# Two hybrid decoder layers on one core: the state-key transposes of layer 0 at one place, the attention's third tile at the place of the spatial gating

## The chip, the core and the metric

The kernel runs on one core of a Trainium2 chip. In this kernel TensorE (PE in the profile) does the matrix products and transposes, with results in PSUM; VectorE (DVE) and ScalarE (ACT) take them from there and do the elementwise work; GpSimd (POOL) has small operations on statistics; SyncE (SP) issues the DMAs. The metric is the device time of one execution in microseconds. Before the change the median of three runs is 1480.12 us (1479.88 to 1480.13).

## What is computed

Two decoder layers over one sequence of 2048 tokens, 1024 wide, float32. Layer 0, cut to what matters here:

```python
h = x @ w_in
q, k, v, g_a, a_lr, u, sv, g_b = _split(h, EVEN_SIZES)
log_a = jax.nn.log_sigmoid((a_lr @ w_a2 + b_a).astype(jnp.float32)) / GLA_TAU
o = _gla(...)                                   # gated linear attention, 4 heads, chunks of 64
o_a = _head_rmsnorm(o, gla_norm_g) * jax.nn.silu(g_a)
o_b = _spatial_gating(gelu(u), gelu(sv), ...) * jax.nn.silu(g_b)   # 4 groups, chunks of 128
y = jnp.concatenate([o_a, o_b], axis=-1) @ w_out
x = _layer_norm(DN_ALPHA * x + y, ln_g, ln_b)
```

In the gated linear attention the state that enters a chunk of 64 tokens is the decayed state before it plus a product of keys and values of the chunk before; each chunk also has causal scores of its own. Layer 1 has the same outline with retention and pooling in place of the two branches.

## The kernel before

The sequence is taken in four blocks of 512 tokens (`for b in range(NB)`, line 852), each through layer 0 and then layer 1. A block is four tiles of 128 tokens, and a tile holds two chunks of the attention.

**The large products.** `unit` (line 164) multiplies the block by 512 columns of a weight matrix. Operands are cut into a high and a low part, and three products of the parts are added (`PASSES`, line 162), so each of the 8 slices of the contraction takes three instructions per result; these are the matmuls of line 181. In most units the work goes in two halves of two results each (width 2): a half is 8 slices by 2 results by 3 passes, 48 matmuls. Each result has one of four PSUM banks named `big`. The weights come by DMA; `cut` (line 114) makes the high part on ScalarE (line 89) and the remainder on VectorE (line 90), and `pace` (line 124) spreads these cuts over the matmuls.

**The small work and its places.** All other work of TensorE is put between the large products by a list of steps. `later(fn, delay)` appends a step; `between()` (line 147) takes one off every delay and runs those that have come to zero, in the order in which they were appended. A unit of width 2 calls `between()` four times: in the middle of its first half, at that half's end once the results have been handed to ScalarE or VectorE, in the middle of the second half and at its end. The text calls these its places 1 to 4. Every engine takes its instructions in the order in which they are written here.

Layer 0 has the units in this order: values (two), q and k, sv, "u and gate" (groups 0 and 1 of the spatial gating), the attention's gate, the rest of u and gate, and then two for the output. The steps around the change:

| step | lines | place before | PSUM that it takes |
|---|---|---|---|
| `state_keys`, pair of heads 0: four transposes, four ScalarE copies | 555 to 560 | q and k, 3 | one `tr` bank |
| `state_keys`, pair of heads 1 | 555 to 560 | sv, 1 | one `tr` bank |
| `first`: scores and chunk states of tile 0 | 422 | sv, 2 | two `s` banks, two `tr` banks |
| `outputs(0)` | 428 | sv, 3 | the same |
| `outputs(1)` | 428 | u and gate, 1 | the same |
| `outputs(2)`, the third tile | 428 | u and gate, 3 | the same |
| `sgu(0)`, `sgu(1)`, the spatial gating's first products | 625 | u and gate, 4 | one `tr` bank each |
| `outputs(3)` | 428 | attention's gate, 1 | two `s` banks |
| `out` of heads 0 and 1 | 653 | attention's gate, 2 | one `tr` bank each |

`outputs(t)` writes the products of tile t, then the scores and the chunk states of tile t + 1 (line 442). The chunk states lie in two banks u[0] and u[1] from `tr()`. `carry_on` (line 410) then adds them to the running states with four VectorE sums (line 414) that read u[0], u[1], u[0], u[1] in this order. Behind them come the norm (ScalarE squares of line 583, a VectorE sum of line 585, GpSimd's power of line 201), `prepare` (lines 418 and 575) and the scaling (line 591).

`sgu(g)` (line 625) takes a bank from `tr()`, fills it with four float32 products that have the normalised `zt` as weights (line 629, two instructions each), and then has three VectorE operations, the second of which reads that bank (lines 630 to 634).

There are **two banks** behind `tr()`:

```python
    ps_tr = ctx.enter_context(tc.tile_pool(name="ps_tr", bufs=2, space=PSUM))
```

A third request must wait until the last reader of the bank that comes round again is done; the framework puts that wait on the TensorE instruction that first writes it.

In block 0 alone, `angles(2)` (line 327) spreads 21 operations of the rotary tables over seven places, three at each, from sv, place 2, to "u and gate", place 4. The sixth group, at place 3 of "u and gate", is a clamp on VectorE, a sine on ScalarE that reads it and a negation on VectorE.

Of the kernel before, what the change touches and what calls it, by code (L numbers as in the profile page):

```python
# [51 lines left out]
def trunk(ctx, tc, x, xT, pos, wv, w, w_a2, pvec, rowp, sgu_rows, w_sT, w_pool, ropec, poolc, out):  # L52
# [24 lines left out]
    def tr():  # L77
        return ps_tr.tile([P, 4, P], F32, tag="tr", name="trp")
# [65 lines left out]
    def later(fn, delay=1):  # L144
        steps.append([delay, fn])
# [112 lines left out]
    s0 = const.tile([P, 2, P], F32, name="s0")  # L258
# [29 lines left out]
    for kt in range(KT):  # L288
# [4 lines left out]
        t = wpool.tile([P, 2, 512], F32R, tag="w", name="wt")  # L293
# [64 lines left out]
    def half(n):  # L358
        return slice(64 * n, 64 * n + 64)
# [3 lines left out]
    def by_heads(copy, dst, src):  # L363

        for r in range(2):
            for c in range(2):
                copy(r, dst(r, c), src(c, r))
# [10 lines left out]
    def attend(qk, kt, vt, state, upd, norm, delays):  # L378

        states = [state, s_odd]

        def mm(dst, lhsT, rhs, start=False, stop=False):
            nc.tensor.matmul(dst, lhsT=lhsT, rhs=rhs, start=start, stop=stop, skip_group_check=True)  # L385

        def banks():

            return [ps_s.tile([P, 4, P], F32, tag="s", name="att") for _ in range(2)]

        def vals(t, s, r, c):
            return vt(t)[half(r), (2 * c + s) * P:(2 * c + s + 1) * P]

        def scores(t, ps, start):
            for c in range(2):
                for s in range(2):
                    for r in range(2):
                        k, q = qk(s, 64 * r, t)
                        mm(ps[r][half(r), 2 + c, half(s)], k[:, half(c)], q[:, half(c)],
                           start=start and c == 0 and s == 0, stop=True)  # L400

        def chunk_states(t):
            u = [tr(), tr()]
            for s in range(2):
                for c in range(2):
                    for r in range(2):
                        mm(u[r][half(c), s, :], kt(s, r, c, t), vals(t, s, r, c), start=s == 0, stop=True)
            return u

        def carry_on(t, u):  # L410
            after = states[(t + 1) % 2]
            for dst, src, c in ((s_mid, states[t % 2], 0), (after, s_mid, 1)):
                for r in range(2):
                    nc.vector.tensor_tensor(dst[half(r)], src[half(r)], u[r][half(c), 0:2, :], op=ALU.add)

        def prepare(t, ps):
            for r in range(2):
                nc.vector.copy_predicated(pm[t % 2][half(r)], mask_b[half(r)],
                                          ps[r][half(r), 2:4, :].rearrange("p c (s i) -> p (c s) i", i=64))
            upd(t, states[(t + 1) % 2])  # L420

        def first():
            ps = banks()
            scores(0, ps, True)
            carry_on(0, chunk_states(0))
            prepare(0, ps)

        def outputs(t):
            m, ps = pm[t % 2], banks()
            last = t == NT - 1  # L430
            for s in range(2):
                for c in range(2):
                    for r in range(2):
                        mm(ps[r][half(c), s, :], m[half(r), 2 * c + s, :], vals(t, s, r, c), start=s == 0)
            for s in range(2):
                for c in range(2):
                    for r in range(2):
                        mm(ps[r][half(c), s, :], qk(s, 64 * r, t)[1][:, half(c)],
                           (states[t % 2], s_mid)[c][half(r), s, :], stop=True)
            if not last:  # L440
                scores(t + 1, ps, False)
                carry_on(t + 1, chunk_states(t + 1))
            scale = norm(t, [p_[:, 0:2, :] for p_ in ps])
            if not last:
                prepare(t + 1, ps)
            scale()

        later(first, delays[0])
        for t in range(NT):
            later(lambda t=t: outputs(t), delays[t + 1])  # L450
# [40 lines left out]
    def layer0(b, xs):  # L491

        vt = r8.tile([P, NT, 512], F32, tag="r8", name="v0")
# [49 lines left out]
        def evac_qk(n, ps):  # L543
            held[n] = ps
            if n % 2 == 0:
                return
            s = n // 2
            psq, psk = held[n - 1], ps

            G = r8.tile([P, 3, TB], F32, tag="r8", name=f"G{s}")  # L550
            e, ei, _ = decays[s]
            nc.vector.tensor_tensor(G[:, 1, :], psk, ei, op=ALU.mult)
            nc.vector.tensor_tensor(G[:, 0, :], psq, e, op=ALU.mult)

            def state_keys():
                pt = tr()
                for t in range(NT):
                    nc.tensor.transpose(pt[:, t, :], G[:, 1, t * P:(t + 1) * P], ident)  # L558
                kt4 = G[:, 2, :].rearrange("p (t c i) -> p t c i", c=2, i=64)
                by_heads(act_copy, lambda r, c: kt4[half(r), :, c, :], lambda c, r: pt[half(c), :, half(r)])  # L560

            later(state_keys, 2)
            heads[s] = G

        unit(xs, evac_qk, False)

        def qk(s, b0, t):
# [25 lines left out]
            return scale  # L593


        attend(qk, kt, lambda t: vt[:, t, :], s0, upd, norm, (2, 3, 5, 7, 9))
        if b == 0:
            angles(2)
        zt = z8.tile([P, NT, 512], F32, tag="z8", name="zt")
# [252 lines left out]
    for b in range(NB):  # L852
        x1, rows = layer0(b, list(xunits))
        layer1(b, x1, rows)
# [68 lines left out]
```

## Time and profile before

| | |
|---|---|
| median of three runs | 1480.12 us |
| the profiled execution's own time | 1480.69 us |
| its span, first to last instruction | 1479.0 us |
| granted TensorE clock, mean | 0.997 |
| busy: PE, DVE, ACT, POOL | 99%, 67%, 40%, 7% of the span |
| line 181 on PE, all 6144 matmuls | 725.2 + 625.7 us of modelled busy time |
| DMA | 162.35 MB, mean 110 GB/s |

A PE matmul is recorded with a modelled end, and matmuls overlap, so the busy share says little about the rate. The chain of waits is of more use: it cuts overlapping matmuls at the start of the next and gives the time for which each kind of work held the path to the end. In its rows stand the start, the length, the engine, the tile written, the line and the number of instructions. A row of the timeline gives start, length, engine, line, operation, written and read tile, and in brackets the engine's idle time before it with what ended it.

### The profile page before, as it was taken

What the parts mean: (1) busy time and instruction counts of PE and PEld (TensorE: products, weight loads), DVE (VectorE), ACT (ScalarE), POOL (GpSimd) and SP (SyncE); (2) the same over time, 40 slices, a digit from 0 to 9 for tenths busy, and PEclk for the clock granted to TensorE, in tenths of its full rate; (3) what the DMA queues carried; (4) which work ended last, traced back from release to release, by engine and by line L of the source; (5) the groups of instructions that cost most, each with busy time, mean ns of one, the idle gap of its engine ahead of it and who ended that gap; (6) DMA issues with size and microseconds to landing.
All of it is one profiled execution on the core that took longest, in us unless ns stands there. A gap on an engine that the chain in (4) does not pass through costs nothing.

```text
span 1479.0 us, 23323 instructions
## 1 busy us (share of the span) xinstructions
PE 1463.8 (99%) x8752; PEld 1224.1 (83%) x8752; DVE 989.7 (67%) x2056; ACT 595.6 (40%) x1116; POOL 101.0 (7%) x137
## 2 busy tenths in 40 slices
PE   8999999999999999999999999999999999999997
PEld 7888888888988888888898888888889888888886
DVE  5596586757657458676756746967675664696755
ACT  6534424243653332434274342334327434143430
POOL 1010010100001001000100100000010010000001
PEclk9999999999999999999999999999999999999999
DMA  7324423115513341313452243132434325222321
GB/s 240 101 77 152 129 71 111 62 58 173 200 58 114 116 142 57 115 58 98 146 185 86 87 142 114 59 114 75 129 120 164 100 73 175 82 93 80 103 77 57
DMA packets 87057, 162.35 MB, mean 110 GB/s; under 512 B 10096, under 2 KB 18336, under 8 KB 86944
## 3 DMA queue, kind: packets, MB, share of 16 engines
q1 hardware_dynamic: 86944, 160.85, 34.2%
q8 instruction: 69, 1.13, 0.3%
q14 instruction: 44, 0.36, 0.1%
HBM read 152.43 MB, written 8.39 MB: 109 GB/s over the span
## 4 chain that ended last, share of the span: by engine, by line
PE 98%; issue 0%; DVE 0%; DMA 0%; ACT 0%; POOLq 0%; POOL 0%; DVEq 0%; ACTq 0%
PE big L181 89%; PE att L385 3%; PE trp L385 1%; PE trp L629 1%; PE trp L681 1%; PE trp L781 1%; PE trp L656 0%; PE trp L821 0%; PE trp L721 0%; PE trp L558 0%; DMA xraw<-in_xT 0%; PE trp L458 0%; PE trp L514 0%; POOLq L919 0%; POOL lnrs L201 0%
## 5 line engine op out<-in xcount | busy, mean ns | idle before, releaser
L181 PE MATMUL big<-wt,T 128*128 128x512 f32 (+2 forms) x3456 | 725.2, 369 | 6.7 <-ACT wt L89 4.5
L181 PEld LDWEIGHTS big<-wt,T 128*128 128x128 f32 x3456 | 599.1, 190 | 112.3 <-ACT wt L89 4.5
L181 PE MATMUL big<-T,wt 128*128 128x512 f32 x2688 | 625.7, 391 | 0.0
L181 PEld LDWEIGHTS big<-T,wt 128*128 128x128 f32 x2688 | 500.6, 188 | 107.7 <-issue 5.4
L90 DVE TENSOR_TENSOR wt<-raw,wt 128x512 fp32r<-128x512 f32 (+1 forms) x496 | 315.5, 673 | 215.5 <-ACT wt L89 215.1
L89 ACT ACTIVATE wt<-raw 128x512 fp32r<-128x512 f32 (+1 forms) x496 | 296.6, 615 | 312.4 <-PE big L181 214.3
L201 POOL TENSOR_TENSOR lnrs<-lnrs,neghalf 128x1 f32<-128x1 f32 x32 | 40.8, 1275 | 628.0 <-DVE lnrs L198 628.0
L219 DVE SCALAR_TENSOR_TENSOR rows<-rows,big 128x512 f32<-128x512 f32 x64 | 43.6, 682 | 53.1 <-PE big L181 53.1
L370 ACT ACTIVATE v<-big 64x128 f32<-64x128 f32 (+1 forms) x184 | 56.8, 309 | 36.2 <-PE big L181 20.8
L201 POOL TENSOR_TENSOR rs<-rs,neghalf 128x4 f32<-128x4 f32 x48 | 48.9, 1018 | 239.1 <-DVE rs L198 236.5
L683 ACT ACTIVATE T<-trp 128x512 fp32r<-128x512 f32 x32 | 17.4, 596 | 105.6 <-PE trp L681 105.6
L231 DVE SCALAR_TENSOR_TENSOR rows<-rows,lnrs,ln 128x1024 f32<-128x1024 f32 (+1 forms) x36 | 41.6, 1166 | 11.4 <-POOL lnrs L201 10.6
L220 DVE BATCH_NORM_STATS2 lnst<-rows 128x6 f32<-128x512 f32 x64 | 44.5, 695 | 2.2
L228 DVE SCALAR_TENSOR_TENSOR rows<-rows,lnmv,ln 128x1024 f32<-128x1024 f32 x32 | 40.9, 1277 | 0.0
L789 ACT ACTIVATE pb<-big 128x512 f32<-128x512 f32 x16 | 9.6, 600 | 76.7 <-PE big L181 76.2
L90 DVE TENSOR_TENSOR T<-y,T 128x512 fp32r<-128x512 f32 x48 | 31.7, 690 | 12.2 <-ACT T L89 11.7
L641 ACT ACTIVATE act<-big 128x512 f32<-128x512 f32 x32 | 18.3, 598 | 51.2 <-PE big L181 50.5
L607 DVE BATCH_NORM_STATS2 st<-zt 128x6 f32<-128x128 f32 x64 | 13.9, 279 | 35.1 <-ACT zt L603 35.1
L206 DVE SCALAR_TENSOR_TENSOR y<-trp,pv,sg 128x512 f32<-128x512 f32 x48 | 33.7, 745 | 4.4 <-PE trp L656 4.4
L796 DVE TENSOR_TENSOR pl<-pb 128x527 f32<-128x527 f32 x16 | 11.3, 705 | 30.0 <-ACT pb L789 29.9
L89 ACT ACTIVATE T<-y 128x512 fp32r<-128x512 f32 x48 | 28.9, 626 | 6.0 <-DVE y L206 5.7
L90 DVE TENSOR_TENSOR T<-xraw,T 128x512 fp32r<-128x512 f32 x32 | 21.2, 685 | 13.3 <-ACT T L89 13.3
(197 smaller groups left out, 960.6 us busy)
## 6 DMA issues: line engine op xcount, KB each, us to landing
raw<-in_w SPq DMA_DIRECT2D x448, 256.0 KB, 2.9
xraw<-in_xT SPq DMA_DIRECT2D x32, 256.0 KB, 3.1
rows<-in_x SPq DMA_DIRECT2D x8, 1024.0 KB, 7.2
ln<-in_rowp SPq DMA_DIRECT2D x16, 512.0 KB, 6.0
out<-rows SPq DMA_DIRECT2D x12, 512.0 KB, 2.7
raw<-in_wv SPq DMA_DIRECT2D x32, 136.0 KB, 3.0
raw<-in_wv SPq DMA_DIRECT2D x32, 128.0 KB, 2.8
out<-rows SPq DMA_DIRECT2D x8, 256.0 KB, 2.0
```

Of the source, the lines that this page charges most:

```text
L89: nc.scalar.activation(hi, src, AF.Copy)
L90: nc.vector.tensor_tensor(lo, src, hi.bitcast(F32), op=ALU.subtract)
L181: nc.tensor.matmul(p_, lhsT=lhsT, rhs=rhs, start=(kt == 0 and q == 0), stop=(kt == KT - 1 and q == 2))
L201: nc.gpsimd.tensor_tensor(dst, dst, neghalf[:, :n], op=ALU.pow)
L206: nc.vector.scalar_tensor_tensor(y, psT, gain, sil, op0=ALU.mult, op1=ALU.mult)
L219: nc.vector.scalar_tensor_tensor(rh, rh, ALPHA, ps, op0=ALU.mult, op1=ALU.add)
L220: nc.vector.bn_stats(sts[t][:, half, :], rh)
L228: nc.vector.scalar_tensor_tensor(row, row, mv[:, 0:1], gt, op0=ALU.subtract, op1=ALU.mult)
L231: nc.vector.scalar_tensor_tensor(row[:, cs], row[:, cs], rs, bt[:, cs], op0=ALU.mult, op1=ALU.add)
L370: nc.scalar.activation(dst, src, AF.Copy)
L385: nc.tensor.matmul(dst, lhsT=lhsT, rhs=rhs, start=start, stop=stop, skip_group_check=True)
L641: nc.scalar.activation(dst, ps, AF.Silu if kind == "g" else AF.Gelu_apprx_tanh)
```

## The change

```diff
@@ layer0, evac_qk
-            later(state_keys, 2)
+            later(state_keys, 4 - 2 * s)
@@ layer0
-        attend(qk, kt, lambda t: vt[:, t, :], s0, upd, norm, (2, 3, 5, 7, 9))
+        attend(qk, kt, lambda t: vt[:, t, :], s0, upd, norm, (2, 3, 5, 8, 9))
```

No operation is added or removed. For the first pair of heads (s = 0) the state keys get a delay of 4 in place of 2: they leave "q and k", place 3, and come to sv, place 1, directly ahead of those of the second pair, whose delay stays 2. The five delays given to `attend` are those of `first` and of `outputs(0)` to `outputs(3)`; the fourth goes from 7 to 8, so `outputs(2)` leaves "u and gate", place 3, and comes to place 4. There it was appended before `sgu(0)` and `sgu(1)`, so it runs ahead of them (in block 0 with the seventh group of `angles` between). Layer 1 calls `attend` with delays of its own and is not touched.

## The prediction

> **What bounds the kernel now.** I read the page's busy times first, then the list of who waited for whom, cut to TensorE, then the chain of waits in block 1, where the change sits.
>
> ```profile
> PE 1463.8 (99%) x8752; PEld 1224.1 (83%) x8752; DVE 989.7 (67%) x2056; ACT 595.6 (40%) x1116; POOL 101.0 (7%) x137
> ...
> PE 98%; issue 0%; DVE 0%; DMA 0%; ACT 0%; POOLq 0%; POOL 0%; DVEq 0%; ACTq 0%
> ```
>
> ```profile
> PE big L181 <- ACT wt L89: 4.5, 1, 4.5
> PE big L181 <- DVE v L373: 2.1, 2, 1.1
> PE trp L458 <- DVE cst L325: 0.4, 1, 0.4
> PE big L181 <- DVE wt L90: 0.2, 1, 0.2
> ```
>
> TensorE holds 98% of the path to the end, and all its waits for other engines come to 7.2 us, in five pieces. So a microsecond of TensorE work that is saved comes off the end, and a microsecond for which TensorE is made to wait is added to it, since no later wait is there to absorb it. The four other engines matter only through the waits that they cause.
>
> ```profile
> 418.51 0.44 PE trp L558 x4
> 418.94 10.91 PE big L181 x48
> 429.86 0.44 PE trp L558 x4
> ...
> 468.58 1.42 PE att L385 x45
> ...
> 470.51 5.66 PE big L181 x24
> 476.18 1.78 PE trp L629 x16
> 477.96 5.46 PE big L181 x24
> ```
>
> This is the path in block 1. Rows of L558 are the state keys, first at "q and k", place 3, then at sv, place 1. At 468.58 the third tile starts (u and gate, place 3), and at 476.18 the spatial gating's products (place 4), 5.66 us of large products later. No row of another engine stands between: TensorE goes through all places without a stop.
>
> **The state keys.** The change moves four transposes, 0.44 us, to a place that already has four. What could be saved is the cost of one visit. The rows show none: four transposes hold the path for 0.44 us, 0.11 us each, and the 48 large products behind them take 10.91 us, where twice the undisturbed 5.46 us for 24 (477.96) is 10.92. So moving them gives 0.0 us. What hides the copies:
>
> ```profile
> 430.33 1.55 ACT L370 ACTIVATE G<-trp 64x256 f32<-64x256 f32 x4 [5.25 <-PE trp L558]
> ...
> 435.14 1.28 ACT L603 ACTIVATE zt<-big 128x512 f32<-128x512 f32 x2 [1.96 <-PE big L181]
> ```
>
> ScalarE stood idle for 5.25 us before the second pair's copies and for 1.96 us before its next evacuation. Four more copies, 1.55 us, start as early and fit into the 1.96 us, so that evacuation isn't late, and the chunk states of `first`, which need both pairs' copies and both `tr` banks, come after that evacuation's large products. If that cover were gone, the price would be at most the 1.55 us per block; I take nothing. At "q and k", place 3, ScalarE gets 1.55 us back, which nobody waits for.
>
> **The third tile at place 4.** On TensorE the same instructions are issued in another order. The visit of the attention costs something at its exit: 24 large products take 5.66 us behind it and 5.46 us behind the spatial gating, 0.20 us more. In the new order the spatial gating's products stand behind the attention and would pay that 0.20 us in the large products' place. So without any wait the sum is 0.0 us, and at best 0.20 us per block less.
>
> But place 4 now asks for four `tr` banks where there are two: u[0] and u[1] for the chunk states of tile 3, then one each for `sgu(0)` and `sgu(1)`. The first product of `sgu(0)` must wait until u[0] has been read for the last time, by the third of the four sums of L414.
>
> ```profile
> 470.44 5.73 PE L181 MATMUL big<-T,wt 128*128 128x512 f32 x24
> ```
>
> ```profile
> 469.28 0.69 DVE L90 TENSOR_TENSOR wt<-raw,wt 128x512 fp32r<-128x512 f32 x1 [0.66 <-ACT wt L89]
> 470.56 0.86 DVE L414 TENSOR_TENSOR s_mid<-s_odd,trp 64x256 f32<-64x256 f32 x2 [0.60 <-PE trp L385]
> 471.46 0.88 DVE L414 TENSOR_TENSOR s<-s_mid,trp 64x256 f32<-64x256 f32 x2
> ...
> 474.49 0.76 DVE L591 TENSOR_TENSOR v<-att,rs 128x256 f32<-128x256 f32 x2
> ```
>
> At today's place the instruction behind the chunk states starts at 470.44, 1.86 us after the visit began. The sums start at 470.56; the third is the first half of the row at 471.46 and ends at 471.46 + 0.44 = 471.90. Today these banks are next wanted by the spatial gating at 476.18, so nobody waits. How a wait of this kind ends is shown by the one that the trace has, at block 0's constants, where a `tr` bank is asked for while VectorE still reads it:
>
> ```profile
> 36.14 0.69 DVE L325 TENSOR_TENSOR cst<-trp,sgubs 128x512 f32<-128x512 f32 x1 [0.85 <-PE trp L324]
> 36.88 0.18 PEld L458 LDWEIGHTS trp<-alrT,wa 48*128 48x128 f32 x1 [0.67 <-DVE cst L325]
> 36.88 0.50 PE L458 MATMUL trp<-alrT,wa 48*128 48x512 f32 x1 [0.35 <-DVE cst L325]
> ```
>
> VectorE ends at 36.83 and TensorE goes on at 36.88, 0.05 us later. So the spatial gating starts at 471.95 in place of 470.44: **1.51 us** of wait. `sgu(1)` needs u[1], free 0.44 us later, while `sgu(0)` itself takes half of 1.78 us: no second wait. The weight load waits too, since it starts at 36.88 with its matmul; the 0.20 us therefore stays behind the wait. [...] Its ends: 1.31 us by the best exit above, and 2.20 us if one remainder of a cut (0.69 us) lies before the sums. Today the remainder before them ended 0.60 us before they could start; the cuts follow the large products' own steps, place 4 has the same distance to them as place 3, and so I take 1.51 us for blocks 1, 2 and 3: 4.53 us.
>
> What is queued behind: on TensorE the spatial gating and all large products; on VectorE the norm, `prepare` and the scaling of tile 2, then the spatial gating's operations. The fourth tile needs the scaling done, which ends at 475.25, 6.67 us after the visit began. In the new order its visit comes 1.86 + 1.51 + 1.78 + 5.46 = 10.6 us after, so the shorter distance costs nothing.
>
> **Block 0** differs, since VectorE is behind there with the rotary tables.
>
> ```profile
> 103.98 1.42 PE att L385 x45
> ```
>
> ```profile
> 108.72 0.85 DVE L414 TENSOR_TENSOR s_mid<-s_odd,trp 64x256 f32<-64x256 f32 x2
> ...
> 113.29 0.42 DVE L333 TENSOR_SCALAR ang<-ang 128x512 f32<-128x512 f32 x1
> ...
> 114.93 2.50 DVE L90 TENSOR_TENSOR wt<-raw,wt 128x512 fp32r<-128x512 f32 x4 [0.76 <-ACT wt L89]
> 117.35 0.68 DVE L333 TENSOR_TENSOR kk<-kk,ang 128x512 f32<-128x512 f32 x1
> ```
>
> The third tile started at 103.98, yet its sums started at 108.72, without a pause on VectorE before them. With `outputs(2)` gone from place 3, the clamp (113.29 today) takes that slot, 108.72. The four remainders follow it by 1.64 us (113.29 to 114.93, as ScalarE first takes the sine), so 110.36, and the next operation follows by 2.42 us: the sums start at 112.78. The third ends 1.34 us after the first begins (470.56 to 471.90), at 114.12, and TensorE goes on at 114.17. It would have been there at 103.98 + 5.46 + 1.86 = 111.30. The wait is **2.87 us**; its ends are 1.51 us, as in the other blocks, and 4.27 us, if the sums lag as far behind TensorE as today (from 103.98 + 1.86 to 108.72, 2.88 us, and then 1.34 and 0.05). I take the reckoned value, as each of its steps is a row of this stretch.
>
> The waits sum to 4.53 + 2.87 = 7.40 us.
>
> **The clock.** A wait of this length may do more than its own time:
>
> ```profile
> 20.20 0.59 PE L181 MATMUL big<-wt,T 128*128 128x256 f32 x3 [1.01 <-DVE v L373]
> 21.89 2.51 PE L181 MATMUL big<-wt,T 128*128 128x256 f32 x14 [1.10 <-DVE v L373]
> ```
>
> ```profile
> 22.00:24.00 2.00, 2.00 (x14) 2.00 (x15) 1.25 (x7) 0.60 (x3) 1.03 (x4) 0.72 0.93 266
> 24.00:26.00 2.00, 2.00 (x11) 2.00 (x11) 1.36 (x5) 1.99 (x6) 0.00 (x0) 0.50 0.98 317
> 26.00:28.00 2.00, 2.00 (x17) 2.00 (x17) 2.00 (x4) 0.58 (x2) 0.00 (x0) 0.92 0.63 212
> ```
>
> After two waits of 1.01 and 1.10 us with 0.59 us of work between, the granted clock (the third number from the end) fell to half: for 2 × 0.28/0.5 = 1.12 us of the first stretch, all of the second and 0.32 us of the third, 3.44 us in all. Work at half rate for 3.44 us loses 1.72 us. Block 0's 2.87 us is more idle time than the 2.11 us that brought this about; 1.51 us is less. So I count one such drop, in block 0: 7.40 + 1.72 = 9.12 us. Against the profiled execution's own 1480.69 us that is 1489.8 us. The median of the runs lies 0.57 us below that execution, at 1480.12 us, so **1489.2 us**.
>
> **Rivals.** The clock holds: only a longer pause lowers it, the waits alone count, 7.40 us, 1487.5 us. For it: the one drop came after two pauses, and no row shows that a single one brings it about. Against it: 2.87 us is longer than both together. [...]
>
> The clock drops in several blocks: 1.51 us suffices, at up to 1.72 us each. All four: 7.40 + 4 × 1.72 = 14.3 us, 1494.4 us. For it: nothing in the trace shows that 1.51 us is too little. Against it: the only drop seen came after 2.11 us.
>
> Not slower: the wait is covered, and the exit of the attention goes from the path, since the spatial gating's weight loads lie under it. That gives 4 × 0.20 = 0.8 us, 1479.3 us. It decides if the wait per block is under 0.20 us, so if the sums of u[0] were over by the time the chunk states' last products are issued. Against it: the sums can't start before those products (470.56 against 470.44), and three of them take 1.34 us.
>
> A knock-on: VectorE's later work, 1.5 to 2.9 us of TensorE's time closer together, makes a later place wait too. If each block lost its copies' 1.55 us once more on top of the forecast, 1489.2 + 6.2 = 1495.4 us. The 10.6 against 6.67 us above speak against it.
>
> **Chances.** Forecast 0.45, clock holds 0.25, clock drops in several blocks 0.17, not slower 0.08, knock-on 0.05. The range goes from waits at their low end, 4 × 1.31 = 5.2 us, 1485.3 us, to the lower clock in every block, 1494.4 us; the last two cases are left out. About 0.2% (3.0 us) is what a measurement of this kernel can tell from no change. All cases but one are slower by more; the one is 0.06 for no change and, as the exit could be worth more than seen, 0.02 for faster.
>
> **What would show it.** In the profile after, the chain at place 4 of "u and gate" should have a VectorE row of L414, near 1.4 us, between the attention and L629, in each block, and the list of waits a row of L629 waiting for L414, four times, some 7 us in total, the longest in block 0; the granted clock should show one stretch of half rate near 114 us. The state keys should be eight transposes of 0.87 us at one place with no wait at `first`. I am wrong if L629 starts within 0.2 us of the chunk states' end, if the wait in blocks 1 to 3 is over 2.2 us, or if the time moves by another wait than this.

## The result and the profile after

The kernel after takes 1489.68 us, median of four runs (1487.67 to 1490.55), against 1480.12 us before: a ratio of 1.0061, with a 95% interval of 1.0049 to 1.0072. It is slower by 9.6 us. The profiled execution is the one of 1490.55 us, with a span of 1488.8 us; it lies 9.86 us above the profiled execution of before (1480.69 us).

Busy time and the shares of the chain by engine, from the page:

```profile
PE 1466.1 (98%) x8752; PEld 1226.1 (82%) x8752; DVE 990.3 (67%) x2056; ACT 595.3 (40%) x1116; POOL 101.0 (7%) x137
...
PE 95%; DVE 3%; DMA 1%; issue 1%; ACT 0%; POOLq 0%; POOL 0%; DVEq 0%; ACTq 0%
```

The instruction counts are those of before. What is new is that VectorE holds 3% of the path to the end, where it held none. That share, some 40 us, isn't the loss: in block 0 the chain, once it has reached VectorE, goes back almost entirely on that engine from 113.58 to 70.69 us, where VectorE is behind, and 36 us of the share lie there. What TensorE lost is read from its waits. The list of waits, for TensorE alone, names the place (columns: total us, times, longest):

```profile
PE trp L629 <- DVE s L414: 7.4, 4, 2.8
PE big L181 <- ACT wt L89: 4.4, 1, 4.4
PE big L181 <- DVE v L373: 1.8, 2, 1.1
PE big L181 <- DVE wt L90: 0.7, 2, 0.5
PE trp L458 <- DVE cst L325: 0.4, 1, 0.4
```

The first row is the only new one: the spatial gating's products wait for the sums of L414, once per block, 7.4 us in all. In the chain of waits of block 1 it looks like this:

```profile
479.25 1.42 PE att L385 x45
480.67 0.02 PE trp L385
480.69 0.06 PE att L385 x2
480.75 0.51 PE trp L385 x14
481.26 0.39 DVE s_mid L414
481.65 0.03 issue
481.68 0.43 DVE s_mid L414
482.11 0.02 issue
482.13 0.43 DVE s L414
482.56 0.14 issue
482.70 2.02 PE trp L629 x16
484.72 5.50 PE big L181 x24
```

The path leaves TensorE behind the last chunk state, goes through exactly three sums and comes back. The third is the last reading of u[0]; the fourth isn't on the path. The 0.20 us that the large products paid behind the attention is now paid by the spatial gating: its 16 instructions hold 2.02 us (1.78 before), and the 24 large products 5.50 us (5.66 before).

In block 0 the granted clock also falls. The windows of the kernel after (the third number from the end is the clock):

```profile
112.00:116.00 4.00, 2.28 (x11) 2.31 (x12) 3.50 (x8) 2.33 (x5) 0.77 (x2) 0.63 0.73 243
116.00:120.00 4.00, 4.00 (x14) 3.42 (x14) 3.89 (x8) 0.63 (x1) 0.43 (x1) 0.51 0.04 14
120.00:124.00 4.00, 4.00 (x19) 3.05 (x17) 2.23 (x4) 0.00 (x0) 0.00 (x0) 1.00 0.00 0
```

That is 4 × 0.37/0.5 + 4 × 0.49/0.5 = 6.9 us at half rate; the trace's clock record has 0.50 from 113.06 to 119.88 us. What it costs stands in the chain of block 0:

```profile
113.72 3.75 PE trp L629 x16
117.47 6.63 PE big L181 x24
```

These forty instructions hold 10.38 us here and 2.02 + 5.50 = 7.52 us in block 1: 2.86 us for the clock. In blocks 1 to 3 it stays at full rate in this execution, 1.00 from 124 to 1485 us.

The start also took a little less than in the profiled execution of before: the drop of the clock at 22 to 26 us that the prediction shows isn't in this one, which was granted 1.00 from 20 to 28 us. The same eight instructions in the chain of the kernel after, and of the kernel before:

```profile
34.75 0.91 PE trp L324 x8
```

```profile
35.20 0.91 PE trp L324 x8
```

The sum of this execution: 7.4 us of waits, 2.9 us for the clock in block 0, and 0.45 us less at the start. That is 9.85 us, and 9.86 us were measured.

### The profile page after: what moved, and what is told of

The parts are those of the page before. It is cut to its first block, busy times and chain, and to the rows that moved or that the text cites. A ratio compares the mean times of both kernels' runs of the same rounds, so it can differ in the third digit from the quotient of the medians.

```text
span 1488.8 us, 23321 instructions
## 1 busy us (share of the span) xinstructions
PE 1466.1 (98%) x8752; PEld 1226.1 (82%) x8752; DVE 990.3 (67%) x2056; ACT 595.3 (40%) x1116; POOL 101.0 (7%) x137
## 4 chain that ended last, share of the span: by engine, by line
PE 95%; DVE 3%; DMA 1%; issue 1%; ACT 0%; POOLq 0%; POOL 0%; DVEq 0%; ACTq 0%
PE big L181 86%; PE att L385 3%; PE trp L629 1%; PE trp L681 1%; PE trp L385 1%; PE trp L781 1%; DMA raw<-in_w 1%; DVE wt L90 1%; PE trp L821 0%; PE trp L721 0%; PE trp L656 0%; DVE s_mid L414 0%; DVE ang L333 0%; DVE zt L616 0%; PE trp L558 0%
## 5 line engine op out<-in xcount | busy, mean ns | idle before, releaser
L90 DVE TENSOR_TENSOR wt<-raw,wt 128x512 fp32r<-128x512 f32 (+1 forms) x496 | 316.3, 671 | 222.1 <-ACT wt L89 221.5
L90 DVE TENSOR_TENSOR T<-y,T 128x512 fp32r<-128x512 f32 x48 | 31.7, 689 | 12.2 <-ACT T L89 11.8
L583 ACT ACTIVATE sq<-att 128x256 f32<-128x256 f32 x32 | 10.6, 385 | 56.2 <-PE att L385 56.2
```

The source lines that it names most:

```text
L90: nc.vector.tensor_tensor(lo, src, hi.bitcast(F32), op=ALU.subtract)
```

## The experiments

The theory after the result: all of the loss comes from the two transpose banks, named `tr` in the program. The wait for them is set by the third sum, and block 0's wait, the only one over 2 us, lowers the clock as well. The rivals: the order or the number of visits on TensorE costs by itself, moving the keys has a part in it, or the clock falls for another reason in block 0. Each experiment is told with its edit, against the kernel before in the first two and against the full change in the others.

**The keys alone.**

```diff
-            later(state_keys, 2)
+            later(state_keys, 4 - 2 * s)
```

> Only the first line of the change: the state keys of both pairs at one place, the third tile where it was. If a visit of TensorE costs only its own transposes, as the 0.44 us for four and 0.87 us for eight say, this is no change: 1480.1 us, within 0.5 us, with no wait at the tile's first step. The rival, that each visit has a cost beyond its instructions, gives 0.2 us or more per block less, 1479.3 us or lower. If the eight copies in a row made ScalarE late, up to 1.55 us per block more, 1486 us.

1480.43 us (11 runs) against 1480.40 us (21 runs): ratio 1.0000, 0.9991 to 1.0009. In the chain of block 1 the eight transposes stand at one place:

```profile
429.56 0.87 PE trp L558 x8
430.44 5.47 PE big L181 x24
435.90 0.55 PE att L385 x13
```

Eight take 0.87 us, two visits of four took 2 × 0.44 us, and the tile's first step follows without a wait. Merging two visits of this kind gives nothing.

**The tile alone.**

```diff
-        attend(qk, kt, lambda t: vt[:, t, :], s0, upd, norm, (2, 3, 5, 7, 9))
+        attend(qk, kt, lambda t: vt[:, t, :], s0, upd, norm, (2, 3, 5, 8, 9))
```

> Only the second line of the change: the third tile at the place of the spatial gating, the state keys where they were. If the wait for the two transpose banks is the whole loss, the time of the full change comes back: 1487.5 us with the clock held, 1489 to 1490.6 us with a clock drop in block 0, and the list of waits shows L629 behind L414 four times, about 7.4 us. If moving the keys had part in it, it lies between.

1489.47 us (1487.57 to 1490.27), ratio 1.0057, 1.0045 to 1.0070: the time of the full change. The list of waits:

```profile
PE trp L629 <- DVE s L414: 7.4, 4, 2.9
```

Its profiled execution took 1487.68 us, and there the clock held in block 0, although the wait was as long:

```profile
112.00:116.00 4.00, 2.43 (x19) 2.36 (x20) 3.50 (x9) 2.17 (x5) 0.93 (x2) 1.00 0.76 258
116.00:120.00 4.00, 4.00 (x19) 3.29 (x18) 3.90 (x8) 0.63 (x1) 0.27 (x1) 1.00 0.00 0
```

So this execution shows the waits alone: 1480.40 + 7.4 = 1487.8 us. The second edit is the whole loss. The scatter of 1487.6 to 1490.3 us goes with the clock: the two short runs (1487.57 and 1487.68 us) have a mean granted clock of 0.998, the three long ones 0.996 to 0.997. Only one of them was profiled.

**Other banks for the spatial gating.** The wait is taken away by giving `sgu(0)` and `sgu(1)` other banks, with the order unchanged:

```diff
-            pt = tr()
+            pt = big().rearrange("p (t c) -> p t c", c=P) if g < 2 else tr()
```

> The full change, but the spatial gating's first two products take two of the four banks of the large products in place of the transpose banks. The theory: no wait of L629 for L414, no clock drop in block 0, and the time is back near 1480.1 us; in block 0 the next large products may wait up to 1.1 us for ScalarE's evacuation, since their banks are now the two last used: 1480 to 1481.3 us. The rival, that the order itself costs (the spatial gating's products directly behind the attention's), leaves it near 1487.5 us.

1480.97 us (1480.66 to 1481.43, 11 runs), ratio 1.0004, 0.9995 to 1.0013: not shown to differ from the kernel before. The list of waits has no row of L629; the one new row is the predicted one of block 0, and its 0.5 us is about what the two medians differ by (0.57 us). In the profiled execution the clock holds in block 0: the 24 large products behind that wait hold 5.75 us in the chain, against 6.63 us in the full change. The row of the wait:

```profile
PE big L181 <- ACT act L641: 0.5, 1, 0.5
```

In the chain of block 1 the spatial gating now follows the chunk states without a stop:

```profile
476.02 0.44 PE trp L385 x14
476.46 1.98 PE big L629 x16
478.45 5.47 PE big L181 x24
```

The order itself costs nothing that can be measured, and it gains nothing: the 0.20 us at the attention's exit is still there, in the 1.98 us of L629. Two visits merged per block, with no wait left, are worth nothing that can be measured here.

**Both readings of u[0] first.** This shortens the wait by one sum without removing it:

```diff
-            for dst, src, c in ((s_mid, states[t % 2], 0), (after, s_mid, 1)):
-                for r in range(2):
+            for r in range(2):
+                for dst, src, c in ((s_mid, states[t % 2], 0), (after, s_mid, 1)):
```

> The full change, with the four sums in another order: both readings of u[0] first, then both of u[1]. If the spatial gating waits for the last reading of u[0], its wait shortens by one sum, 0.44 us, in each block: 1.07 us in blocks 1 to 3, 2.44 us in block 0, 5.65 us in all, so 1485.8 us with the clock held and up to 1488.7 us with a drop. If it waits for all four sums or for something else behind them, nothing changes: 1487.5 to 1490.6 us.

1488.08 us (1485.72 to 1488.41), ratio 1.0047, 1.0035 to 1.0060. The list of waits and the chain of block 1:

```profile
PE trp L629 <- DVE s L414: 5.6, 4, 2.4
```

```profile
480.37 0.42 DVE s_mid L414
480.79 0.02 issue
480.81 0.43 DVE s L414
481.25 0.14 issue
481.39 2.04 PE trp L629 x16
```

Two sums on the path in place of three, and 5.6 us in place of 7.4. The wait goes with the last reader of the bank. The waits alone would give 1480.40 + 5.6 = 1486.0 us, near the fastest run, 1485.72 us; the profiled execution, 1488.41 us, has a clock drop in block 0, with 0.79 granted from 112 to 116 us and 0.78 from 116 to 120 us. As a whole this version isn't shown to differ from the full change, since their ranges meet: the 1.8 us saved is smaller than the scatter of its runs.

**Block 0 alone, and blocks 1 to 3 alone.** Two kernels:

```diff
-        attend(qk, kt, lambda t: vt[:, t, :], s0, upd, norm, (2, 3, 5, 8, 9))
+        attend(qk, kt, lambda t: vt[:, t, :], s0, upd, norm, (2, 3, 5, 8 if b == 0 else 7, 9))
```

> The full change, but the third tile moves in block 0 alone; blocks 1 to 3 keep it at its old place. The wait there is 2.9 us: 1483.1 us with the clock held, and up to 1486.0 us where an execution's clock drops behind it, so the runs should scatter by up to 2.9 us. If the scatter comes from the blocks with the short wait, it is gone here and all runs lie at 1483.1 us.

In the second, the 7 and the 8 are exchanged.

> The full change, but in block 0 the third tile stays at its old place. Three waits of 1.5 us: 1480.2 + 4.5 = 1484.7 us, and if 1.5 us is too little to lower the clock, no run is over 1485.6 us, the scatter being that of the kernel before. If such a wait can lower it, runs lie up to 2.9 us per block higher, to 1493 us.

Block 0 alone: 1485.21 us (1484.81 to 1485.41, six runs), ratio 1.0031, 1.0020 to 1.0043. Its profile has one wait of L629:

```profile
PE trp L629 <- DVE s L414: 2.8, 1, 2.8
```

2.8 us give 1483.2 us from the 1480.37 us of before, measured beside it; the median lies 2.0 us higher. In the profiled execution the clock drops for 3.4 us (0.85 granted from 112 to 116 us, 0.73 from 116 to 120 us), and the forty instructions behind the wait show what that cost, 9.14 us against the 7.52 us at full rate:

```profile
114.49 3.49 PE trp L629 x16
117.97 5.65 PE big L181 x24
```

That is 1.6 of the 2.0 us. The expected scatter of 2.9 us didn't come: all six runs lie 1.6 to 2.2 us above the waits alone, so the clock probably dropped in all of them; only one was profiled.

Blocks 1 to 3 alone: 1485.33 us (1484.87 to 1486.90), ratio 1.0034, 1.0021 to 1.0046.

```profile
PE trp L629 <- DVE s L414: 4.5, 3, 1.5
```

Four of the five runs lie at 1484.9 to 1485.5 us, near the waits alone, 1480.37 + 4.5 = 1484.9 us. The fifth, 1486.90 us, was against the expectation; it wasn't profiled, and what made it longer stays open.

**Longer waits in blocks 1 to 3.** Three additions on a spare buffer, whose results nothing reads, delay the sums there; `extra` is a new argument of `attend`, 3 for layer 0 in blocks 1 to 3 and 0 elsewhere. The edit, cut to the loop:

```diff
             after = states[(t + 1) % 2]
+            for _ in range(extra if t == NT - 1 else 0):
+                nc.vector.tensor_tensor(spare, spare, spare, op=ALU.add)
```

> The full change, and in blocks 1 to 3 three idle additions on VectorE (480 columns each, about 0.65 us) ahead of the sums for the last tile, on a spare buffer. Some 0.6 us of them fall into VectorE's idle time, so each of these three waits grows by 1.3 us to 2.8 us: 7.4 + 3.9 = 11.3 us, 1491.5 us with the clock held. If the length of the wait decides over the clock, blocks 1 to 3 now drop as well in part of the executions, at 1.7 to 2.9 us each: a median of 1493 us or more and a scatter over several us, up to 1503 us. If the drop belongs to something else in block 0, the runs lie between 1491.5 and 1494.4 us.

1498.97 us (1498.14 to 1499.41, four runs), ratio 1.0125, 1.0110 to 1.0141. The list of waits, with this kernel's line numbers (L633 is the spatial gating, L417 the sums), and its windows in block 1:

```profile
PE trp L633 <- DVE s L417: 11.2, 4, 2.9
```

```profile
480.00:484.00 4.00, 1.22 (x17) 1.01 (x9) 3.81 (x8) 1.97 (x5) 0.00 (x0) 0.93 0.37 123
484.00:488.00 4.00, 4.00 (x19) 3.71 (x19) 3.86 (x9) 0.00 (x0) 1.20 (x2) 0.64 0.00 0
```

The waits account for 11.2 us of the 18.6 us between the medians. In the profiled execution, 1498.14 us, the clock now drops in each of the four blocks, for 3.4 us at half rate each by the trace's clock records (in block 1 the two windows with 0.93 and 0.64), and the mean granted clock is 0.993, against 0.996 in block 0 alone. It lies 17.8 us above the median of before: 11.2 us of waits and 6.6 us more, some 1.6 us per block, as in block 0 alone. The other three runs are 0.8 to 1.3 us longer and weren't profiled; that part stays open. So a wait of 2.8 us can bring the drop about in blocks 1 to 3 too, and block 0 needs no other cause than the length of its wait.

**The rotary tables later.** In block 0 their last two groups move behind the spatial gating:

```diff
-            later(lambda some=some: [fn() for fn in some], delay)
+            later(lambda some=some: [fn() for fn in some], delay if delay < 7 else delay + 2)
```

> The full change, but in block 0 the last two groups of the rotary tables run two places later, behind the spatial gating's first products. If VectorE's lag behind the sine makes block 0's wait long, it is 1.5 us there as in the other blocks: 4 x 1.5 = 6.0 us, 1486.2 us, and with no wait over 2 us left no clock drop and little scatter. If the lag comes from the earlier groups, the wait stays near 2.9 us: 1487.5 to 1490.5 us.

1486.38 us (1485.97 to 1487.18), ratio 1.0041, 1.0028 to 1.0053. The list of waits and VectorE's timeline in block 0:

```profile
PE trp L629 <- DVE s L414: 6.0, 4, 1.5
```

```profile
105.89 4.90 DVE L90 TENSOR_TENSOR wt<-raw,wt 128x512 fp32r<-128x512 f32 x8
111.00 0.86 DVE L414 TENSOR_TENSOR s_mid<-s_odd,trp 64x256 f32<-64x256 f32 x2 [0.21 <-PE trp L385]
```

With the sine out of the way VectorE is idle when the chunk states end, and block 0 waits 1.5 us like the others. This also settles a rival that the chain of the full change names ahead of ScalarE's cut at 109.20 us, a transfer of weights that landed at 109.07 us: here ScalarE's last cut waits for such a transfer until 109.21 us, and TensorE's wait is short all the same. The clock holds in the profiled execution (1.00 from 108 to 120 us, 0.999 on the mean). 1480.37 + 6.0 = 1486.4 us: the four waits are now the whole loss.

No version beats the kernel before. Of those that move the third tile, the only one that comes level with it takes the wait away by other banks.

## Why the prediction was right

**The bound.** Each microsecond of wait put into TensorE's path appeared at the end: in profiled executions in which the clock held, 7.4 us of waits gave 1487.7 us, 4.5 gave 1484.9 us, 6.0 gave 1486.4 us.

**The state keys.** Forecast 0.0 us; the keys alone measured a ratio of 1.0000. The eight copies started as early behind their transposes as the four did and ended ahead of the next evacuation, with 0.81 us to spare where the four left 1.96 us, as the ScalarE rows of the kernel after show:

```profile
435.15 3.12 ACT L370 ACTIVATE G<-trp 64x256 f32<-64x256 f32 x8 [5.25 <-PE trp L558]
438.29 1.28 ACT L603 ACT_TABLE_LOAD   x1
440.38 1.28 ACT L603 ACTIVATE zt<-big 128x512 f32<-128x512 f32 x2 [0.81 <-PE big L181]
```

**The wait in blocks 1 to 3.** Forecast 1.51 us each, measured 1.5 us, through the third sum, with VectorE free when the sums could start. TensorE goes on 0.14 us behind the third sum in place of 0.05 us, which is too little to tell in the total. That the weight load would wait too, and the 0.20 us stay behind the wait, also held: in block 1 the load starts at 482.67 us, 0.03 us ahead of the first product, and L629 holds 2.02 us.

**Block 0.** The forecast let the clamp take the slot of the sums, put the sums 4.06 us behind it and came to a wait of 2.87 us. VectorE's timeline after:

```profile
108.22 0.42 DVE L333 TENSOR_SCALAR ang<-ang 128x512 f32<-128x512 f32 x1
108.67 0.43 DVE L333 TENSOR_SCALAR kk<-ang 128x512 f32<-128x512 f32 x1
109.85 2.50 DVE L90 TENSOR_TENSOR wt<-raw,wt 128x512 fp32r<-128x512 f32 x4 [0.75 <-ACT wt L89]
112.27 0.85 DVE L414 TENSOR_TENSOR s_mid<-s_odd,trp 64x256 f32<-64x256 f32 x2
```

The sums come 4.05 us behind the clamp, and the wait is 2.8 us. That the lag comes from this group of the tables is shown by the tables moved later. All times are some 0.5 us earlier than reckoned, as this execution had the shorter start.

**The clock.** The term was mis-sized. One drop in block 0 was right, but the prediction took 3.44 us at half rate, 1.72 us lost; the profiled execution had 6.9 us and lost 2.86 us. Where the drop lasted 3.4 us, as in block 0 alone, 1.6 us were lost, near the forecast. Nor does each execution pay it: 1487.67 us, the fastest of the four runs, is what the rival gives in which the clock holds (1487.5 us), and the tile alone shows such an execution in profile. Waits of 2.4 to 2.9 us lowered it in the profiles of u[0] first (2.4 us), of the full change and of block 0 alone (2.8 us each) and of the longer waits (up to 2.9 us); in that of the tile alone one of 2.9 us didn't. The forecast of 1489.2 us stood between the two kinds of execution. That it came out within 0.5 us of the median, 1489.68 us, is in part luck.

**The other rivals.** A drop in several blocks didn't come: behind waits of 1.5 us the granted clock was 1.00 in blocks 1 to 3 of the full change and in block 0 of the tables later, and blocks 1 to 3 alone came, with a mean clock of 0.998, to the time of its waits alone; with 2.8 us in each block the drops did come. The case that wasn't slower was wrong in its gain as well: without the wait the exit of the attention still costs its 0.20 us. No knock-on appeared: the list of waits has no further new row, and the 0.5 us by which the row of L90 grew is a wait that ends at 27 us, in the start.

## What to carry over

Before work of one engine is put together at one place, count the buffers that the steps there ask for: here two steps that each fitted into two PSUM banks needed four when put side by side, and the price is read in the trace of before, from the end of the writer to the last reader of the bank. Merging visits pays only if a visit costs something beyond its instructions, which the rows behind the visit show. Here TensorE's pauses of 2.4 us and more could cost more than their length, and those of 1.5 us weren't seen to, so the longest wait is the first to shorten.

## What the hardware showed beside this

Behind the longer waits the lower clock lasted 3.4 us in the profiled executions of u[0] first, of block 0 alone and of the longer waits, and 6.8 us in that of the full change, and a wait of 2.9 us could pass without it, in the tile alone.

The moment of the fall differs as well. In the kernel after, TensorE paused from 110.88 to 113.72 us, and the clock fell at 113.06 us, 2.2 us into the pause. In the kernel before, the pauses of 1.01 and 1.10 us ended at 20.20 and 21.89 us, and the clock fell at 22.90 us, 1.0 us after the second. The same two pauses in the kernel after, 0.71 and 1.09 us long, passed at a granted clock of 1.00. The clock records of these two profiles begin at 9.24 us of the span before and at 10.66 us after. From there the changes are 13.65, 3.41 and 1447.25 us apart before and 102.40, 6.83 and 1365.33 us after, which are 4, 1, 424, 30, 2 and 400 times 3.4133 us. What sets these distances, and why one wait of 2.9 us lowers the clock and another doesn't, no run shows.
